# Scan outputs of two strips in one block, and the samples' memory values with exchanged operands

## The chip, the cores and the metric

The kernel runs on one core of a Trainium2 chip. The metric is the device time of one launch in microseconds (us), the median of several runs; smaller is better. A profile of one execution gives a trace of every engine: TensorE (PE, its weight loads PEld), VectorE (DVE), ScalarE (ACT), GpSimd (POOL) and the DMA queue of SyncE (SP).

## What is computed

One layer of a streaming encoder over 288 tokens (256 of a prompt, 32 of a sample), model width 2048: an RMS norm, one large projection, three branches (sparse attention, a Mamba-2 scan, cross-attention into 256 memory tokens), each gated and projected, their sum through an output matrix, a last norm. Two pieces matter here, cut from the reference:

```python
# the scan, chunks of up to 64 tokens, 32 heads of 64 in 4 groups, state 128
wgt = cb[..., None] * jnp.exp(seg) * dtc[:, :, None]
y_diag = jnp.einsum('bclsgr,bcsgrp->bclgrp', wgt, x)               # inside a chunk
y_off = jnp.einsum('bclgn,bcgrpn,bclgr->bclgrp', cc, h_in, jnp.exp(cum))   # from the state
y = y_diag + y_off
...
# memory attention
s = jnp.einsum('bthd,bmhd->bhtm', qh, mk) * (M_HEAD_DIM ** -0.5)
p = jax.nn.softmax(s, axis=-1)
o = jnp.einsum('bhtm,bmhd->bthd', p, mv)                           # the memory values
```

## The kernel before

**The stream.** Nearly all of the work is a stream of large products. A strip is 128 output channels; its weights come in halves of [128, 8, 128], loaded on SP's queue (line 183), split into a high part on ScalarE (line 186) and a low part on VectorE (line 187), and multiplied with the 288 tokens in 24 matmuls of 288 columns for a half (`strip`, `ps` tiles in PSUM). The order of the halves is a list, `jobs`, and `run` walks it: convert a later half, emit this half's matmuls, call `step`.

**Side work.** Everything else (attention, scan, scores) is written as generators. `step`, called after each half, advances the active ones to their next `yield`; at most `width` of them are active, others wait in `queue` in their order. So what a generator emits between two yields stands in each engine's queue between one half's matmuls and the next one's, as one block. Nothing reorders queues at run time but the waits. Side work uses PSUM tiles of the kind `sd` (five) and SBUF tiles of the kind `t2` (six).

**The scan** (`scan(g)`, one generator for each of four groups, one active at a time) holds the prompt's 256 tokens in two column blocks of 128 and the sample's 32 in a third (`COLS`). `Lt` has the masked decays, `xdt` the tokens' inputs, `hh` two states (for the prompt's second block, and for the sample), `C_` the output vectors. A group has four strips of 128 channels, two heads each. `out(j)` (lines 917 to 927) makes one strip's outputs in one PSUM tile: columns 0 to 288 from `xdt` and `Lt`, by block and head (64 output channels each, so half of the array's columns; for the third block only 32 of its rows), and columns 288 to 448 from `hh` and `C_`, with all 128 channels at once. `put(j)` (lines 929 to 934) reads them on VectorE and GpSimd. The calls: `out(0)`, `out(1)`, a yield, `put(0)`, `put(1)`, `out(2)`, `out(3)`, a yield, `put(2)`, `put(3)` and the states.

**The samples' memory attention** (`m_sample`, lines 456 to 481) has scores of four heads in four 32-row parts of one tile, a softmax, a transpose to `pt`, and then the values: for each head and each half of its 256 channels two accumulating matmuls with 128 channels of the cached values as weights and 32 columns of `pt` moving. Line 480 copies the result to `OTm`. It is one of the pieces that start behind the memory queries; the step sizes (`g_misc`), the index scores (`score`, two PSUM tiles for a pair of heads, read by line 590), `score_sample` and `select` follow in the queue, two active at a time.

An fp32 matmul of the program appears in the trace as two loads and two matmuls, one of fp32r (the stream) as one of each.

Of the kernel before, what the change touches and what calls it, by code (L numbers as in the profile page):

```python
# [9 lines left out]
AF = mybir.ActivationFunctionType  # L10
# [3 lines left out]
P = 128  # L14
# [9 lines left out]

# column blocks of the combined projection, in the order in which the kernel walks them
N_MQ, N_IQ, N_AK, N_AV, N_AQ, N_MZ, N_XBC, N_G = 8, 8, 2, 2, 8, 8, 24, 16
# [7 lines left out]
def step_kernel(ctx, tc, ins, outs):  # L34
# [17 lines left out]
    def sd():  # L52
        return psum.tile([P, 512], F32, tag="sd", bufs=5, name="sd")

    def t2(n=512):
        return tmp.tile([P, n], F32, tag="t2", name="t2")
# [10 lines left out]
    def mm(out, lhsT, rhs, start=True, stop=True):  # L67
        PE.matmul(out, lhsT, rhs, start=start, stop=stop)  # L68

    # ------------------------------------------------------------------ loads of the start  # L70
    N = Names()
# [27 lines left out]

    # ------------------------------------------------------------------ norms  # L100
    def rsqrt(v, p, n, size):
        """v = 1/sqrt(p / size + EPS), [128, n]; p in PSUM."""
        r, u = t2(n), t2(n)
        S.activation(r, p, AF.Ln, scale=1.0 / size, bias=eps)  # L104
        V.tensor_scalar(v, p, 1.0 / size, EPS, OP.mult, OP.add)
        S.activation(r, r, AF.Exp, scale=-0.5)
        V.scalar_tensor_tensor(u, r, -0.5, r, OP.mult, OP.mult)
        V.tensor_tensor(u, u, v, OP.mult)
        V.scalar_tensor_tensor(v, u, 1.5, r, OP.add, OP.mult)
# [14 lines left out]

    # ------------------------------------------------------------------ the streamed products
    jobs = []          # halves: (dram ap, shape, matmul emitter)
    conv = []          # converted halves that wait for their products
    state = {"c": 0}

    def strip(halves, mov, evac, n=T):  # L130
        """One block of 128 output channels; halves of its weights [128, 8, 128]."""
        box = {}
        for j, ap in enumerate(halves):
            def go(wh, wl, j=j):
                hi, lo = getattr(N, mov) if isinstance(mov, str) else mov
                if j == 0:
                    box["p"] = ps()
                p = box["p"][:, 0:n]
                k0 = 8 * j
                last = j == len(halves) - 1  # L140
                for i in range(8):
                    mm(p, wh[:, i], hi[:, k0 + i], j == 0 and i == 0, False)
                    mm(p, wh[:, i], lo[:, k0 + i], False, False)
                for i in range(8):
                    mm(p, wl[:, i], hi[:, k0 + i], False, last and i == 7)
                if last:
                    evac(p)
            jobs.append((ap, [P, 8, P], go))
# [20 lines left out]
    def hook(f):  # L169
        """f is called between the products before and after it."""  # L170
        jobs.append((None, None, f))
# [17 lines left out]

    # ------------------------------------------------------------------ side work  # L190
    queue, active = [], []
# [8 lines left out]
    def turn(key, gap):  # L200
        """Waits until gap halves have passed since the turn before this one."""
        while clock["t"] < clock.get(key, 0):
            yield
        clock[key] = clock["t"] + gap


    def later(*fs):
        """Each of fs one half further on than the one before it."""
        chains.append(list(fs))
# [44 lines left out]

    # ------------------------------------------------------------------ memory keys and values
    N.mkT = slot("E", [P, 8, 256])
# [109 lines left out]

    # ------------------------------------------------------------------ projections of the step
    wi = {"s": 0}
# [40 lines left out]

    # ---- memory attention  # L410

    def softmax(p, c, width_, scale):
        """Rows of p [128, c * width_]: c softmaxes; the maximum is subtracted."""
        m = st()
        V.tensor_reduce(m[:, 0:c], p.rearrange("p (i k) -> p i k", i=c), AX.X, OP.max, negate=True)
        V.tensor_scalar(m[:, 2:2 + c], m[:, 0:c], scale, None, OP.mult)
        e = t2()[:, 0:c * width_]
        for i in range(c):
            a = slice(i * width_, (i + 1) * width_)
            S.activation(e[:, a], p[:, a], AF.Exp, scale=scale, bias=m[:, 2 + i:3 + i],  # L420
                         accum_out=m[:, 4 + i:5 + i])
        V.reciprocal(m[:, 6:6 + c], m[:, 4:4 + c])
        for i in range(c):
            a = slice(i * width_, (i + 1) * width_)
            V.tensor_scalar(e[:, a], e[:, a], m[:, 6 + i:7 + i], None, OP.mult)
        return e
# [29 lines left out]
    def m_sample():  # L456
        p = sd()[:, 0:256]
        for h in range(4):
            for e in range(2):
                mm(p[32 * h:32 * h + 32], N.mqT[:, 2 * h + e, TP:T], N.cmk[:, 2 * h + e], e == 0, e == 1)  # L460
        yield
        e = softmax(p, 1, 256, 1.0 / 16)
        yield 2
        q = sd()[:, 0:256]
        for k in range(2):
            PE.transpose(q[:, k * P:k * P + P], e[:, k * P:k * P + P], ident)
        yield
        pt = t2()[:, 0:256]
        S.activation(pt, q, AF.Copy)
        yield  # L470
        o = sd()
        for h in range(4):
            for d in range(2):
                j = 2 * h + d
                for k in range(2):
                    c = h * 256 + d * P
                    mm(o[:, 32 * j:32 * j + 32], N.cmv[:, k, c:c + P], pt[:, k * P + 32 * h:k * P + 32 * h + 32],
                       k == 0, k == 1)
        yield
        S.activation(N.OTm[:, :, TP:T], o[:, 0:256].rearrange("p (j t) -> p j t", j=8), AF.Copy)  # L480
        mark("m")
# [7 lines left out]

    # ---- index keys, index weights, step sizes  # L490
    wt = const.tile([P, 3, 64], F32, name="wt")
# [13 lines left out]

    # columns of dts: step sizes, their products with -exp(a_log), running sums
    dt = const.tile([P, 96], F32, name="dt")
# [5 lines left out]
    def g_misc():  # L513
# [13 lines left out]
        mark("misc")  # L527
        # log(1 + exp(u)) = max(u, 0) + 2 atanh(e / (2 + e)), e = exp(-|u|)
        V.scalar_tensor_tensor(e, u, -1.0, u, OP.mult, OP.max)
# [40 lines left out]

    # ---- index scores
    def begin_a():
# [5 lines left out]
    def score(j):  # L578
        yield from need("misc")
        # a pair of heads, each in its own half of the rows of the array  # L580
        ps_ = [sd(), sd()]
# [104 lines left out]

    # ---- memory branch output
    def ev_mz(j, p):
# [12 lines left out]

    # ------------------------------------------------------------------ convolution, attention
    ASC = 128 ** -0.5
# [69 lines left out]
    cso = const.tile([P, 24, 6], F32, name="cso")  # L773
    # strips: the first group's channels, B, C, the other groups' channels
    order = list(range(4)) + list(range(16, 24)) + list(range(4, 16))
# [32 lines left out]

    # ------------------------------------------------------------------ memory gate; the scan
    def begin_scan():  # L810
# [14 lines left out]
    def scan(g):  # L825
# [28 lines left out]
        yield  # L854
        # x, token-major, times the step size
        px = []
# [16 lines left out]

        # decays from s to t
        def decay(*rs):
# [37 lines left out]
        yield 2  # L913
        # outputs
        po = []

        def out(j):
            p = sd()
            s = 4 * g + j
            po.append(p)  # L920
            for i, (c0, c1, n) in enumerate(COLS):
                for e in range(2):
                    r = 2 * j + e
                    mm(p[64 * e:64 * e + 64, c0:c1], xdt[0:n, i, 64 * r:64 * r + 64], Lt[0:n, r, c0:c1])
            cs = slice(P * s, P * s + P)
            mm(p[:, 288:416], hh[:, 0, cs], C_[:, 128:256])
            mm(p[:, 416:448], hh[:, 1, cs], C_[:, 256:288])

# [6 lines left out]

        out(0)
        out(1)
        yield
        put(0)
        put(1)  # L940
        ds = [ddx(1), ddx(2)]
        out(2)
        out(3)
        yield
# [24 lines left out]

    # ------------------------------------------------------------------ attention output  # L970
    def ev_az(j, p):
# [8 lines left out]

    # ------------------------------------------------------------------ scan output
    def begin_y():
# [76 lines left out]

    # ------------------------------------------------------------------ output product, last norm  # L1060
    POOLED = (2, 6, 9, 12, 14)
# [134 lines left out]
```

## Time and profile before

| | us |
|---|---|
| median of 3 runs | 1377.06 |
| lowest and highest run | 1375.69, 1378.71 |
| profiled execution: its span, first to last instruction | 1374.1 |

The profile gives no other time of that execution than its span. How to read it: an engine's busy time is the union of its instructions; matmuls are pipelined, so their durations overlap, and the distance between their starts is what one costs. A shape such as `128*64 128x128` is the used part of the array (rows times columns) and the moving data (partitions x columns). Times in a timeline are from the span's start; a row that merges several instructions carries the shape of the first. What stands in brackets is the idle time of the engine before, and what ended it.

### The profile page before, as it was taken

How to read it: one execution, taken by the hardware profiler on the slowest of the kernel's cores; microseconds unless marked ns; L12 is line 12 of the kernel's file. 1: busy time of each engine (PE TensorE's matmuls, PEld its weight loads, DVE VectorE, ACT ScalarE, POOL GpSimd, SP SyncE). 2: the span in 40 equal slices, each digit the busy share in tenths (PEclk: the TensorE clock that was granted, in tenths of full speed). 3: DMA queues.
4: the chain of work that ended last, by engine and by line, in shares of the span. 5: the costliest groups of instructions: out<-in, count | busy, mean ns of one | idle time of the engine just before them, and what ended most of it. 6: DMA issues, size and time to landing. Idle time of an engine off the chain costs nothing.

```text
span 1374.1 us, 24380 instructions
## 1 busy us (share of the span) xinstructions
PE 1347.9 (98%) x10032; PEld 1315.0 (96%) x10032; DVE 770.0 (56%) x1166; ACT 606.4 (44%) x858; POOL 237.5 (17%) x319
## 2 busy tenths in 40 slices
PE   6999999999999999999999999999999999999995
PEld 6989999899999999999999999999999999999995
DVE  7674344594567766646556556663344334555444
ACT  5654343444555543725425336663333433334331
POOL 5501000000000001122231233410044000000433
PEclk9999999999999999999999999999999999999998
DMA  8667434344444445654545445445456555455552
GB/s 288 212 217 255 143 130 132 118 162 158 165 139 151 151 156 164 224 181 146 179 136 186 165 156 167 159 164 172 166 170 218 173 169 166 157 169 169 170 169 84
DMA packets 63006, 232.03 MB, mean 169 GB/s; under 512 B 7264, under 2 KB 7808, under 8 KB 61744
## 3 DMA queue, kind: packets, MB, share of 16 engines
q1 hardware_dynamic: 57888, 209.72, 46.2%
q0 software_dynamic: 4144, 19.30, 4.3%
q8 instruction: 78, 1.28, 0.4%
q10 hardware_dynamic: 864, 1.47, 0.3%
q14 instruction: 32, 0.26, 0.1%
HBM read 223.06 MB, written 7.33 MB: 168 GB/s over the span
## 4 chain that ended last, share of the span: by engine, by line
PE 98%; DVE 1%; DMA 1%; ACT 0%; issue 0%; DVEq 0%; SPq 0%; ACTq 0%
PE ps L68 91%; PE sd L68 6%; DMA A<-in_memT 1%; DVE A L1089 0%; PE sd L861 0%; DVE C L268 0%; PE sd L727 0%; PE sd L845 0%; PE sd L440 0%; DVEq L1174 0%; ACT B L267 0%; ACT F L314 0%; PE sd L671 0%; ACT t L104 0%; ACT t L590 0%
## 5 line engine op out<-in xcount | busy, mean ns | idle before, releaser
L187 DVE TENSOR_TENSOR wl<-wr,wh 128x1024 fp32r<-128x1024 f32 x394 | 493.4, 1257 | 392.0 <-ACT wh L186 391.2
L68 PE MATMUL ps<-xh,wh 128*128 128x288 f32 x2128 | 582.2, 299 | 0.0
L68 PE MATMUL ps<-xl,wh 128*128 128x288 f32 x2128 | 574.5, 296 | 0.0
L186 ACT ACTIVATE wh<-wr 128x1024 fp32r<-128x1024 f32 x394 | 411.9, 1054 | 239.4 <-PE ps L68 194.8
L68 PEld LDWEIGHTS ps<-xh,wh 128*128 128x128 f32 x2128 | 400.3, 188 | 7.1 <-issue 3.4
L68 PEld LDWEIGHTS ps<-xl,wh 128*128 128x128 f32 x2128 | 400.6, 188 | 1.3 <-issue 0.7
L68 PE MATMUL ps<-xh,wl 128*128 128x288 f32 x2128 | 324.5, 294 | 0.0
L68 PEld LDWEIGHTS ps<-xh,wl 128*128 128x128 f32 x2128 | 296.6, 188 | 0.0
L68 PE MATMUL ps<-B,wh 128*128 128x288 f32 (+1 forms) x384 | 102.9, 296 | 9.3 <-ACT wh L186 9.3
L68 PEld LDWEIGHTS ps<-B,wh 128*128 128x128 f32 x384 | 74.2, 193 | 9.3 <-ACT wh L186 9.3
L68 PE MATMUL ps<-E,wh 128*128 128x288 f32 x256 | 70.2, 302 | 0.0
L68 PE MATMUL ps<-F,wh 128*128 128x288 f32 x256 | 69.5, 296 | 0.0
L68 PE MATMUL ps<-A,wh 128*128 128x288 f32 x256 | 69.2, 299 | 0.0
L68 PE MATMUL ps<-mgl,wh 128*128 128x288 f32 x256 | 69.1, 296 | 0.0
L68 PE MATMUL ps<-mgh,wh 128*128 128x288 f32 x256 | 69.0, 295 | 0.0
L790 POOL COPY cso<-t 128x3 f32<-128x3 f32 x24 | 5.0, 210 | 256.9 <-ACT t L788 256.9
L68 PEld LDWEIGHTS ps<-E,wh 128*128 128x128 f32 x256 | 48.3, 189 | 1.0 <-issue 0.8
L68 PEld LDWEIGHTS ps<-F,wh 128*128 128x128 f32 x256 | 48.1, 188 | 0.2 <-issue 0.2
L68 PEld LDWEIGHTS ps<-A,wh 128*128 128x128 f32 x256 | 48.3, 189 | 0.0
L68 PEld LDWEIGHTS ps<-mgl,wh 128*128 128x128 f32 x256 | 48.2, 188 | 0.0
L68 PEld LDWEIGHTS ps<-mgh,wh 128*128 128x128 f32 x256 | 48.1, 188 | 0.0
L68 PE MATMUL ps<-A,wl 128*128 128x288 f32 x256 | 39.3, 296 | 0.0
(290 smaller groups left out, 1348.5 us busy)
## 6 DMA issues: line engine op xcount, KB each, us to landing
wr<-in_w_in SPq DMA_DIRECT2D x266, 512.0 KB, 3.4
wr<-in_w_pb SPq DMA_DIRECT2D x32, 512.0 KB, 3.7
wr<-in_w_o SPq DMA_DIRECT2D x32, 512.0 KB, 3.3
wr<-in_w_mk SPq DMA_DIRECT2D x16, 512.0 KB, 3.8
wr<-in_w_mv SPq DMA_DIRECT2D x16, 512.0 KB, 4.3
wr<-in_w_pm SPq DMA_DIRECT2D x16, 512.0 KB, 3.3
wr<-in_w_pa SPq DMA_DIRECT2D x16, 512.0 KB, 3.3
B<-scr POOLq DMA_DIRECT2D x4, 1152.0 KB, 9.4
```

What stands on the lines that cost most here:

```text
L68: PE.matmul(out, lhsT, rhs, start=start, stop=stop)
L186: S.activation(wh, raw, AF.Copy)
L187: V.tensor_tensor(wl, raw, wh.bitcast(F32), OP.subtract)
L790: G.tensor_copy(cso[:, c, 0:3], u[:, 256:259])
```

## The change

In `scan`, `out` takes two strips: it first takes both PSUM tiles, then for each strip the first two blocks of `Lt` and, by heads, the state's outputs, with 64 weight columns instead of 128, and then for both strips the third block. In `m_sample` the weights of the value matmuls are now 32 columns of `pt` and the moving data 256 channels of the cached values, each head in its own 32 rows of the result; a copy to SBUF, a yield, two transposes, a yield and a rearranging copy bring it to the old form. Other lines of the diff only take comments away.

```diff
@@ m_sample
-        o = sd()
-        for h in range(4):
-            for d in range(2):
-                j = 2 * h + d
-                for k in range(2):
-                    c = h * 256 + d * P
-                    mm(o[:, 32 * j:32 * j + 32], N.cmv[:, k, c:c + P], pt[:, k * P + 32 * h:k * P + 32 * h + 32],
-                       k == 0, k == 1)
-        yield
-        S.activation(N.OTm[:, :, TP:T], o[:, 0:256].rearrange("p (j t) -> p j t", j=8), AF.Copy)
+        o = sd()[:, 0:256]
+        for k in range(2):
+            for h in range(4):
+                a = k * P + 32 * h
+                mm(o[32 * h:32 * h + 32], pt[:, a:a + 32], N.cmv[:, k, 256 * h:256 * h + 256], k == 0, k == 1)
+        yield
+        u = t2()[:, 0:256]
+        S.activation(u, o, AF.Copy)
+        yield
+        q = sd()[:, 0:256]
+        for d in range(2):
+            PE.transpose(q[:, d * P:d * P + P], u[:, d * P:d * P + P], ident)
+        yield
+        S.activation(N.OTm[:, :, TP:T].rearrange("p (h d) t -> p d h t", d=2),
+                     q.rearrange("p (d h t) -> p d h t", d=2, h=4), AF.Copy)
...
@@ scan
-        def out(j):
-            p = sd()
-            s = 4 * g + j
-            po.append(p)
-            for i, (c0, c1, n) in enumerate(COLS):
+        def out(*js):
+
+            for j in js:
+                po.append(sd())
+            for j in js:
+                for i, (c0, c1, n) in enumerate(COLS[0:2]):
+                    for e in range(2):
+                        r = 2 * j + e
+                        mm(po[j][64 * e:64 * e + 64, c0:c1], xdt[:, i, 64 * r:64 * r + 64], Lt[:, r, c0:c1])
+                for w, o, c0, c1 in ((0, 288, 128, 256), (1, 416, 256, 288)):
+                    for e in range(2):
+                        a = P * (4 * g + j) + 64 * e
+                        mm(po[j][64 * e:64 * e + 64, o:o + c1 - c0], hh[:, w, a:a + 64], C_[:, c0:c1])
+            for j in js:
                 for e in range(2):
                     r = 2 * j + e
-                    mm(p[64 * e:64 * e + 64, c0:c1], xdt[0:n, i, 64 * r:64 * r + 64], Lt[0:n, r, c0:c1])
-            cs = slice(P * s, P * s + P)
-            mm(p[:, 288:416], hh[:, 0, cs], C_[:, 128:256])
-            mm(p[:, 416:448], hh[:, 1, cs], C_[:, 256:288])
+                    mm(po[j][64 * e:64 * e + 64, 256:288], xdt[0:32, 2, 64 * r:64 * r + 64], Lt[0:32, r, 256:288])
...
-        out(0)
-        out(1)
+        out(0, 1)
         yield
         put(0)
         put(1)
         ds = [ddx(1), ddx(2)]
-        out(2)
-        out(3)
+        out(2, 3)
```

## Rows read from the trace of the kernel before

**Rows 1.** The page: busy time, share of the span and count of TensorE; the granted TensorE clock in 40 slices of the span, in tenths; and the shares of the engines in the chain of work that ended last.
```profile
PE 1347.9 (98%) x10032; PEld 1315.0 (96%) x10032; DVE 770.0 (56%) x1166; ACT 606.4 (44%) x858; POOL 237.5 (17%) x319
...
PEclk9999999999999999999999999999999999999998
...
PE 98%; DVE 1%; DMA 1%; ACT 0%; issue 0%; DVEq 0%; SPq 0%; ACTq 0%
```

**Rows 2.** The list of waits of TensorE over the whole span: what it waited for, us in total, times, longest.
```profile
PE ps L68 <- ACT wh L186: 9.3, 1, 9.3
...
PE sd L68 <- ACT t L590: 0.5, 1, 0.5
```

**Rows 3.** Busy time by engine in the stretch of the scan: from and to, length, then each engine's busy us and count, granted clock, DMA share, GB/s.
```profile
545.00:770.00 225.00, 225.00 (x1725) 211.11 (x1724) 130.94 (x247) 101.43 (x125) 57.20 (x66) 1.00 0.54 174
```

**Rows 4.** The timeline of TensorE and its weight loads through the first pair of strips, group 0, asked in short stretches so that runs come apart: start, us, what (the first row is the stream's last eight matmuls, the second the eighth of them); then two rows of VectorE from the same time.
```profile
586.12 1.22 PE L68 MATMUL ps<-xh,wl 128*128 128x288 f32 x8
587.05 0.29 PE L68 MATMUL ps<-xh,wl 128*128 128x288 f32 x1
587.27 0.33 PE L68 MATMUL sd<-B 128*64 128x128 f32 x2
587.43 0.39 PE L68 MATMUL sd<-B 128*64 128x128 f32 x4
587.65 0.46 PE L68 MATMUL sd<-B 128*64 128x128 f32 x4
587.86 0.30 PE L68 MATMUL sd<-B 32*64 32x32 f32 x4
587.93 0.23 PE L68 MATMUL sd<-B 32*64 32x32 f32 x2
588.09 0.38 PE L68 MATMUL sd<-G,A 128*128 128x128 f32 x1
588.30 0.42 PE L68 MATMUL sd<-G,A 128*128 128x128 f32 x3
588.41 0.31 PE L68 MATMUL sd<-G,A 128*128 128x32 f32 x2
588.45 0.28 PE L68 MATMUL sd<-G,A 128*128 128x32 f32 x1
588.65 0.33 PE L68 MATMUL sd<-B 128*64 128x128 f32 x2
...
590.15 0.29 PE L68 MATMUL ps<-xl,wh 128*128 128x288 f32 x1
...
587.27 0.14 PEld L68 LDWEIGHTS sd<-B 128*64 128x64 f32 x2 [0.16 <-issue]
587.32 0.25 PEld L68 LDWEIGHTS sd<-B 128*64 128x64 f32 x4
...
588.76 1.22 DVE L187 TENSOR_TENSOR wl<-wr,wh 128x1024 fp32r<-128x1024 f32 x1 [3.29 <-ACT wh L186]
589.90 0.51 DVE L931 SCALAR_TENSOR_TENSOR D<-D,cols,sd 128x288 f32<-128x288 f32 x1
```

**Rows 5.** The timeline of TensorE around the samples' memory values: the last stream matmul before, the values, the second stream matmul after.
```profile
232.00 0.29 PE L68 MATMUL ps<-xh,wl 128*128 128x288 f32 x1
232.13 3.65 PE L68 MATMUL sd<-t,A 128*128 128x32 f32 x32
...
235.84 0.29 PE L68 MATMUL ps<-xl,wh 128*128 128x288 f32 x1
```

**Rows 6.** The timeline of TensorE around the last pair of strips, group 3: the last stream matmul before it and the second after it.
```profile
760.49 0.29 PE L68 MATMUL ps<-xh,wl 128*128 128x288 f32 x1
...
763.60 0.29 PE L68 MATMUL ps<-xl,wh 128*128 128x288 f32 x1
```

**Rows 7.** The timeline of TensorE around the samples' memory scores, and around the two transposes of their softmax, with the stream matmuls before and after each.
```profile
214.09 0.29 PE L68 MATMUL ps<-xh,wl 128*128 128x288 f32 x1
214.32 1.09 PE L68 MATMUL sd<-A,G 128*32 128x256 f32 x16
215.34 0.40 PE L68 MATMUL ps<-xh,wh 128*128 128x288 f32 x1
215.58 0.29 PE L68 MATMUL ps<-xl,wh 128*128 128x288 f32 x1
...
225.40 0.30 PE L68 MATMUL ps<-xh,wl 128*128 128x288 f32 x1
225.53 0.38 PE L466 MATMUL sd<-ident,t 128*128 128x128 f32 x2
225.88 0.29 PE L68 MATMUL ps<-xl,wh 128*128 128x288 f32 x1
```

**Rows 8.** Single lines: the copy of line 469 (durations, first and last start); the last sum of the selection; the first attention head's scores; and two rows of the timeline of TensorE in the half of the last index score.
```profile
L469 ACT ACTIVATE t<-sd x1: 373/373/373, 227.3 to 227.3; 128x256 f32<-128x256 f32 x1
...
L646 DVE TENSOR_TENSOR C<-C x1: 726/726/726, 307.2 to 307.2; 128x544 f32<-128x544 f32 x1
...
357.10 0.82 PE L68 MATMUL sd<-C,B 128*128 128x128 f32 x4
...
263.62 0.49 PE L68 MATMUL sd<-C,B 64*128 64x128 f32 x2
264.57 0.92 PE L68 MATMUL sd<-C,B 64*128 64x128 f32 x6 [0.47 <-ACT t L590]
```

## The prediction

> **What bounds the kernel now.** I read the page's busy times first [rows 1]. TensorE's matmuls are busy 98% of the span, its granted clock is 9 tenths or more in every slice but the last, and the chain of work that ended last is TensorE's for 98%. Then the list of what TensorE waited for [rows 2]: its largest entry is 9.3 us, once, and that lies at the start. In the stretch of the scan it has no idle time at all [rows 3]. So a microsecond that TensorE loses or gains there moves the end by as much, and the other engines matter only where they would make it wait anew.
>
> A busy TensorE need not be a useful one, so the third view is the timeline around the changed steps, read by the starts of matmuls. The stream of 288-column products starts one every 0.133 us (eight from 586.12 to 587.05 [rows 4]). I price a block of side work as the time from the last stream matmul before it to the second one after it, less 0.27 us, which these two would be apart without it.
>
> **One pair of scan strips now.** From 587.05 to 590.15 us [rows 4] is 3.10, so the block costs 2.84 us. Its inside: two matmuls of the 128x64 shape start together every 0.11 us (587.43 to 587.65 is two steps; the first of a block holds 0.16), so both halves of the columns work at once. From the last of them to the first of 32x64 there are 0.20 us, from these to the first of 128x128 0.15. That first one holds 0.21 where later ones hold 0.11 (its load was not ahead), and from the last 32-column one to the next strip's 128x64 there are 0.20. The gaps stand only where the shape of the used part changes: at 232.00 to 232.13 the stream runs into side work of its own shape with no gap [rows 5]. A pair has six such changes. All eight pairs look alike: the last is 760.49 to 763.60, 3.11 [rows 6].
>
> **The pair after.** Per strip, four steps of two matmuls remain for the decayed part, and the state part, four full-width matmuls, becomes eight of half the width: two steps with 128 columns, two with 32. So a pair has 12 steps with 128 columns, 4 with 32, then 4 of 32x64, and three changes of shape. No row shows the 128x64 shape with 32 columns. Below it is bounded by the 0.03 between the 32-column starts at 588.41 and 588.45, above by the 0.11 of 128 columns. I take 0.06, because loads of 64 columns follow each other by 0.05 on each half (587.27 to 587.32) and a matmul can be no faster than its load. From the last stream matmul: 0.22 to the first start, 0.16 for the first step, 11 x 0.11 = 1.21, three 32-column steps 0.18, 0.15 into 32x64 (as after other 32-column matmuls; 0.20 at most), its steps 0.08 + 2 x 0.06, 0.16 to the first stream matmul, and 0.24 to the second (215.34 to 215.58, which follows a change too [rows 7]). That is 2.52, less 0.27: 2.25 us. Saved are 0.59 a pair, **4.7 us** for eight; with the bounds of the five 32-column steps and of the change, 2.3 to 5.9.
>
> Who could take this back? The first strip's outputs now come with the second's, at the end of the block and not in its middle. Their reader on VectorE (line 931) starts at 589.90, behind a weight conversion that began at 588.76 [rows 4]; by the sum the matmuls are over by about 589.5, so nobody waits for that. The masks that the outputs need are a whole half earlier, as now, and no other order of any queue changes here. Loads and conversions run ahead of the products through this stretch, so nothing else becomes late when TensorE needs 0.6 us less a pair.
>
> **The samples' memory values.** Now 32 matmuls with full-width weights and 32 moving columns, 0.11 us each: 232.00 to 235.84, cost 3.57 us [rows 5]. After: 16 matmuls with 32 weight columns in four parts of the array and 256 moving columns. The same function's scores have just this shape and count: 214.09 to 215.58, so 1.22 us. The way back is two transposes, like those at 225.53: 225.40 to 225.88, so 0.21 [rows 7]. Saved: 3.57 - 1.43 = **2.1 us**. The added read of the sums on ScalarE is another copy like line 469's, 0.37 us [rows 8], a half before the transposes need it; ScalarE stands behind no wait of TensorE there. Without that cover it would cost those 0.37.
>
> The generator gets two more yields, so all that queues behind it shifts. The eight index scores wait for its place among the two active pieces: they start two halves later and pack two to a half for one half longer, the later pieces one half later. The margin is large: selection's last sum ends at 307.9, and the first attention head that needs it starts at 357.10 [rows 8]. What can change is how often scores wait for PSUM tiles: at 263.62 one pair of scores began 0.95 us before its other six matmuls, which waited for the read of line 590. With two scores in that half this may come back larger, or disappear; between -0.9 and +0.9 us I take 0.
>
> **Sum.** 4.7 + 2.1 = 6.8 us of 1374.1, the profiled execution's span: 1367.3. The median of the runs stands 3.0 us above that span; nothing in the change touches what lies outside it, so 1377.06 - 6.8 = **1370.3 us**.
>
> **Rivals.**
> Slower: the half-width matmuls of the state part don't overlap, and each must wait for its own load. Its price is 0.21 a matmul, as for the first 128x128 one [rows 4]: per strip 8 x 0.21 = 1.7 instead of 0.34, in 16 strips 22 us, so 1370 + 22 = 1392. It undoes the whole saving from about 0.10 a matmul. For it speaks a change of stationary tensor within one shape, which no row here has. Against it: the loads at 587.32 start while the matmuls of 587.27, in the same 128 rows, still run, and two matmuls start together in each step.
> The Trainium skill says in "TensorE: Matmul & The Clock Gate", section "The mechanism" of Part 3, that a weight load overlaps a running matmul only when it is for another group of rows; by that rule the halves, which use all rows, would pay this price. The overlapping rows just named speak against the rule here, so it gets no more than a small chance.
>
> No gain in the scan: the 0.15 to 0.20 gaps follow the tensors (other weights, other tiles of PSUM) and not the shapes, so regrouping removes none. Then only the memory step gains: 1377.06 - 2.1 = 1375.0, no change that can be measured. Against it is the gapless entry at 232.13, where tile and weights change as well.
>
> Scores wait: the three halves with two scores each wait 0.95 us for PSUM as the one at 263.62 did, where now about half of that much is lost. That costs some 2 us: 1372. For it: the tiles of this kind are five, two scores take four. Against: the list of waits puts only 0.5 us on line 590 in all [rows 2].
>
> **Chances.** Forecast 0.80, scores wait 0.10, no gain in the scan 0.06, slower 0.04. The terms' own bounds give savings from 2.3 + 2.1 - 0.9 = 3.5 to 5.9 + 2.1 + 0.9 = 8.9, so 1368.2 to 1373.6. The ends together are unlikely, but the three runs of before already spread by 3 us: I take 1367.7 to 1373.4. It leaves out the two smallest rivals and little else. A difference of 0.2% (2.75 us) is about what a measurement can tell from none: faster 0.90, same 0.06, slower 0.04.
>
> **What would show it.** In the new profile each pair of strips should last about 2.5 us from the last stream matmul to the second after it, with two 128x64 starts every 0.11 through the state part, and just one 32x64 run. A step of 0.2 there shows the slower rival; a gap between runs of one shape the second. The memory values should be one run of 16 matmuls of 128x32, 1.2 us, and two transposes of 0.2 in a later half. New waits of TensorE for line 590 above 0.5 us would show the third. The prediction is wrong if TensorE gets idle time elsewhere that fills what it saves.

## The result and the profile after

The changed kernel takes **1368.57 us**, the median of four runs (1367.77 to 1369.36), beside 1376.58 for the kernel before (four runs, 1375.69 to 1378.71). The ratio is **0.994** (95% interval 0.9929 to 0.9952): 8.0 us less by the medians. The forecast was 1370.3 in a range of 1367.7 to 1373.4. In five later rounds (the experiment changed_again, below) it gave 0.9941 (0.9929 to 0.9954).

First the page and the list of waits of TensorE, as in [rows 1, 2]. The page's columns are busy time, share and count; the list's are what was waited for, us in total, times, longest.

```profile
PE 1341.2 (98%) x10082; PEld 1310.8 (96%) x10082; DVE 768.8 (56%) x1166; ACT 606.8 (44%) x859; POOL 238.3 (17%) x319
...
PEclk9999999999999999999999999999999999999998
```

```profile
PE ps L68 <- ACT wh L186: 8.5, 1, 8.5
...
PE sd L68 <- ACT t L595: 0.5, 1, 0.5
```

TensorE's busy time fell from 1347.9 to 1341.2 us though it has 50 more matmul passes: 64 more in the scan (the state part in halves), 14 fewer in the memory step. The span fell by 7.5, from 1374.1 to 1366.6. Behind the start no wait was added: the read of the index scores (line 595, formerly 590) still costs 0.5 us once.

The stretch of the scan as in [rows 3] (from and to, length, busy us and count of PE, PEld, DVE, ACT and POOL, granted clock, DMA share, GB/s):

```profile
545.00:770.00 225.00, 225.00 (x1827) 214.17 (x1826) 133.64 (x251) 103.42 (x127) 62.46 (x66) 1.00 0.53 177
```

It is as full as before, at the full clock (1.00 is the 2.4 GHz level). Busy time can't show the gain here; the starts of the matmuls can. The first pair of strips, with the same view and the same ends as in [rows 4], then one row of weight loads and two of VectorE (short stretches, so that runs come apart):

```profile
584.99 0.29 PE L68 MATMUL ps<-xh,wl 128*128 128x288 f32 x1
...
585.59 0.28 PE L68 MATMUL sd<-B 128*64 128x128 f32 x2
585.70 0.28 PE L68 MATMUL sd<-G,A 128*64 128x128 f32 x2
...
585.95 0.23 PE L68 MATMUL sd<-G,A 128*64 128x32 f32 x2
586.01 0.31 PE L68 MATMUL sd<-B 128*64 128x128 f32 x2
...
586.69 0.26 PE L68 MATMUL sd<-G,A 128*64 128x32 f32 x4
586.72 0.23 PE L68 MATMUL sd<-G,A 128*64 128x32 f32 x2
586.88 0.24 PE L68 MATMUL sd<-B 32*64 32x32 f32 x2
...
587.47 0.29 PE L68 MATMUL ps<-xl,wh 128*128 128x288 f32 x1
...
585.59 0.14 PEld L68 LDWEIGHTS sd<-G,A 128*64 128x64 f32 x2
...
586.71 1.23 DVE L187 TENSOR_TENSOR wl<-wr,wh 128x1024 fp32r<-128x1024 f32 x1 [3.29 <-ACT wh L186]
587.85 0.51 DVE L942 SCALAR_TENSOR_TENSOR D<-D,cols,sd 128x288 f32<-128x288 f32 x1
```

From 584.99 to 587.47 is 2.48 us, less 0.27: the block costs 2.21 where it cost 2.84. Two halves start together every 0.11. From the decayed part (out of B) to the state part (out of G, A) and back to the second strip there is no gap of the kind that stands between two shapes: weights, moving data and columns of PSUM change at 585.70 and 586.01, the used part of the array doesn't. One run of 32x64 is left, at the end. The conversion of the weights (line 187) ends at 587.94 by its own row, after the pair's last matmul, and the reader of the outputs (line 942) follows it: nobody waits for the first strip's outputs. There is one small price: the first step of the second strip holds 0.14 us where the others hold 0.11. All eight pairs cost 2.211 to 2.214 (taken with one more digit, where the two stream matmuls would be 0.266 apart).

The memory step, as in [rows 5, 7]: the values, the two transposes that turn them back, and the new copy on ScalarE.

```profile
232.15 0.29 PE L68 MATMUL ps<-xh,wl 128*128 128x288 f32 x1
232.37 1.07 PE L68 MATMUL sd<-A,t 128*32 128x256 f32 x16
...
233.62 0.29 PE L68 MATMUL ps<-xl,wh 128*128 128x288 f32 x1
...
241.25 0.30 PE L68 MATMUL ps<-xh,wl 128*128 128x288 f32 x1
241.38 0.38 PE L482 MATMUL sd<-ident,t 128*128 128x128 f32 x2
241.73 0.29 PE L68 MATMUL ps<-xl,wh 128*128 128x288 f32 x1
...
233.74 0.38 ACT L478 ACTIVATE t<-sd 128x256 f32<-128x256 f32 x1
```

The values cost 1.20 us (232.15 to 233.62, less 0.27) in place of 3.57, the transposes 0.22 (0.48 less 0.27, from starts with one more digit 0.219). The copy is over at 234.12 and the transposes start 7.26 us later.

**Where the time came from.** Eight pairs at 0.631 are 5.05 us, the memory step 3.570 - 1.198 - 0.219 = 2.15, together 7.2. TensorE's stretch, from the first matmul of the prompt's memory scores (160.44 us before, 160.59 after) to the last matmul of all, takes 1191.6 us instead of 1198.9: 7.3 less. The span's other 0.2 is what remains of two differences outside it. The stretch begins 0.15 us later, and behind its end there are 14.4 us instead of 14.8; both of these values come with either form of the kernel (scan_only has 14.4, pair_full_width 14.8). Of the further 0.5 between the span and the medians, 0.3 lies in the part of an execution's time that its span does not hold ("What stays open", below).

### The profile page after: what moved, and what is told of

Read it like the earlier page. It is cut to its first block, busy times and chain, and to the rows that moved or that the text cites. A ratio compares the mean times of both kernels' runs of the same rounds, so it can differ in the third digit from the quotient of the medians.

```text
span 1366.6 us, 24483 instructions
## 1 busy us (share of the span) xinstructions
PE 1341.2 (98%) x10082; PEld 1310.8 (96%) x10082; DVE 768.8 (56%) x1166; ACT 606.8 (44%) x859; POOL 238.3 (17%) x319
## 4 chain that ended last, share of the span: by engine, by line
PE 98%; DVE 1%; DMA 0%; ACT 0%; issue 0%; DVEq 0%; ACTq 0%
PE ps L68 91%; PE sd L68 5%; DVE C L268 0%; DVE A L1098 0%; PE sd L866 0%; DMA cols<-in_cols 0%; PE sd L732 0%; PE sd L850 0%; PE sd L440 0%; DVEq L1183 0%; ACT F L314 0%; PE sd L676 0%; ACT B L267 0%; ACT t L104 0%; ACT t L595 0%
## 5 line engine op out<-in xcount | busy, mean ns | idle before, releaser
(293 smaller groups left out, 1341.2 us busy)
```

## The experiments

Times here are of one run each unless rounds are named; the kernel before ran on the same chip. "Cost" of a block is always the time from the last stream matmul ahead of it to the second behind it, less 0.27 us (0.266 where a third digit is given). None of the kernels leaves out a part of the computation.

### Each part alone

**scan_only** has the new order of the scan's outputs and the old memory values; **mem_only** the reverse. The cut below is of scan_only against the changed kernel; mem_only is the kernel before with the new `m_sample`.

```diff
@@ m_sample
-        o = sd()[:, 0:256]
-        for k in range(2):
...
+        o = sd()
+        for h in range(4):
+            for d in range(2):
...
```

> The scan's part alone, memory values as before. Theory (each block of side work costs TensorE its own time and nothing gives it back): a pair of strips from the last stream matmul to the second one after it, less 0.27 us, 2.21 us as in the changed kernel, eight pairs 5.0 us less than before; the memory values still 3.57; the index scores start in the same halves as before, with TensorE waiting about 0.5 us once for line 590. Rival (the two parts share a gain, for example through the later scores): the pairs differ from 2.21, or the span differs from that of before by clearly more or less than 5 us.

> The memory values' part alone, scan outputs as before. Theory: one block of 16 matmuls for 1.2 us and one with two transposes for 0.22 in place of 3.57, so 2.1 us less; pairs of strips 2.84 as before; the blocks of the step sizes and index scores that shift behind it cost the same in sum within 0.3 us. Rival (scores wait): those blocks cost 1 to 2 us more, and the span gains less than 1 us.

scan_only took 1372.37 us beside 1375.98, mem_only 1373.0. The ends of the first pair of strips in mem_only, on TensorE's timeline:

```profile
584.61 0.29 PE L68 MATMUL ps<-xh,wl 128*128 128x288 f32 x1
...
587.72 0.29 PE L68 MATMUL ps<-xl,wh 128*128 128x288 f32 x1
```

The costs belong to the parts: a pair's ends are 3.11 us apart (cost 2.84) without the new order and 2.48 (2.21) in scan_only; the memory values cost 1.20 in mem_only and 3.57 in scan_only. In mem_only TensorE's stretch (from the prompt's memory scores to the last matmul) is 2.2 us shorter than before's, which is the memory step's 2.15; the blocks of step sizes and scores behind it last the same in sum, within 0.1 us. The rival by which the shifted scores wait falls.

scan_only missed its expected size: TensorE's stretch is 3.6 us shorter, not 5.05. The pairs gained what they should, so 1.5 us were lost elsewhere. They lie behind the memory values: from the first of these to the first matmul of the step sizes there are 8.28 us (232.30 to 240.58), and 6.76 in the kernel before (232.13 to 238.89). The granted clock shows how. Its windows around the old memory values (columns as above), then one of the kernel before behind the same values:

```profile
232.00:236.00 4.00, 4.00 (x37) 4.00 (x36) 3.68 (x9) 1.37 (x3) 0.00 (x0) 1.00 0.26 92
236.20:239.40 3.20, 3.20 (x15) 3.20 (x15) 0.00 (x0) 0.17 (x1) 0.00 (x0) 0.50 0.63 187
239.60:245.00 5.40, 5.40 (x45) 4.95 (x44) 1.22 (x1) 1.06 (x1) 0.00 (x0) 1.00 0.27 97
```

```profile
235.80:239.40 3.60, 3.60 (x30) 3.60 (x29) 0.25 (x1) 1.45 (x2) 0.00 (x0) 1.00 0.58 199
```

TensorE is never idle here, yet right behind the old values the clock stands at 0.50 (the 1.2 GHz level) for 3.4 us: 15 matmuls in 3.20 us where before's profiled execution has 30 in 3.60. This code is the same in both kernels. Whether the old values bring it about is the question of old_values_twice, below.

### What in the pair gains

**halves_one_strip** keeps the halves and gives up putting two strips together.

```diff
-        out(0, 1)
+        out(0)
+        out(1)
...
-        out(2, 3)
+        out(2)
+        out(3)
```

> The changed kernel, but one strip at a time: the state part by halves of the columns, the third block of each strip right behind it. Five changes of shape a pair instead of three (six before). Theory (a change of shape costs what the gaps of before show, the halves' loads are hidden): 2.43 us a pair, so the halves alone give 0.41 of the 0.63 us that a pair gains, taking two strips together 0.22. Rival A (all of the gain is from taking two strips together): 2.8. Rival B (all of it is from the halves): 2.2.

```profile
586.08 0.29 PE L68 MATMUL ps<-xh,wl 128*128 128x288 f32 x1
...
588.79 0.29 PE L68 MATMUL ps<-xl,wh 128*128 128x288 f32 x1
```

1371.26 us, and a pair costs 2.71 - 0.27 = 2.44 (2.446 to 2.454 over the eight). So the halves by themselves save 0.39 a pair, and one run of 32x64 in place of two a further 0.24. Neither of the rivals' values (2.8: only the grouping counts; 2.2: only the halves) came.

**pair_full_width** keeps two strips together and, at the end, the state part in full width, so that there are as few changes of shape as in the changed kernel.

```diff
...
+            for j in js:
+                cs = slice(P * (4 * g + j), P * (4 * g + j) + P)
+                mm(po[j][:, 288:416], hh[:, 0, cs], C_[:, 128:256])
+                mm(po[j][:, 416:448], hh[:, 1, cs], C_[:, 256:288])
```

> The changed kernel with two strips together, but the state part in full width, behind the third blocks: 128x64 for both strips, then 32x64, then 128x128. Three changes of shape, as in the changed kernel, and none into the stream. Theory (changes of shape and loads that are not hidden both count): the first load of 128x128 is exposed once (0.21) and eight full-width loads follow at 0.11 each, 2.45 us a pair. Rival (only the number of changes counts): 2.2 or less, since the change into the stream is gone too.

```profile
586.77 0.29 PE L68 MATMUL ps<-xh,wl 128*128 128x288 f32 x1
...
588.37 1.08 PE L68 MATMUL sd<-G,A 128*128 128x128 f32 x8
...
589.50 0.30 PE L68 MATMUL ps<-xl,wh 128*128 128x288 f32 x1
```

1372.42 us; the pair costs 2.73 - 0.27 = 2.46. The number of shape changes alone does not set the price: eight full-width loads, of which the first is not ahead, cost 0.25 more than the same work in halves, where the 32-column steps come at 0.03 and 0.06.

### The memory step's own questions

**memory_head_outer** puts a head's two steps next to each other, so that four neighbours in the queue no longer lie in four parts of the array.

```diff
-        for k in range(2):
-            for h in range(4):
+        for h in range(4):
+            for k in range(2):
```

> The changed kernel with the loops over heads and halves of the memory exchanged in the memory values: the two accumulating matmuls of a head follow each other, as in the same function's scores. Theory (each of the four column parts takes its own next matmul, whatever stands between in the queue): one block of 1.20 us as in the changed kernel. Rival (matmuls run in the queue's order, so neighbours must lie in different parts to overlap): up to 16 x 0.216 = 3.5 us.

```profile
232.21 0.29 PE L68 MATMUL ps<-xh,wl 128*128 128x288 f32 x1
...
233.70 0.29 PE L68 MATMUL ps<-xl,wh 128*128 128x288 f32 x1
```

1368.37 us; 1.49 - 0.27 = 1.22 us, from starts with one more digit 1.218 beside 1.198. The order costs 0.02 us. The rival of 3.5 (neighbours must lie in different parts) falls.

**no_yield_before_turn** takes away the yield between the copy of the values and their transposes.

```diff
         S.activation(u, o, AF.Copy)
-        yield
         q = sd()[:, 0:256]
```

> The changed kernel without the yield between the copy of the memory values and the two transposes, so that both lie in one half. Theory (the yield hides more than the copy): TensorE waits there for what ScalarE has queued ahead, a weight conversion of 1.05 us, and for the copy of 0.37 us, so the transposes' block costs 0.22 plus 0.4 to 1.8 us; the pieces behind shift by one half less. Rival (only the copy counts, or ScalarE is free): 0.22 to 0.6 us in all.

```profile
233.64 0.38 ACT L478 ACTIVATE t<-sd 128x256 f32<-128x256 f32 x1
...
236.57 0.38 PE L481 MATMUL sd<-ident,t 128*128 128x128 f32 x2
```

1368.18 us, and no wait: the copy is over at 234.02, and the transposes start at 236.57. The half of the stream between the values and the next side work is cover enough. The transposes joined the block of step sizes (1.739 us with them, 1.519 alone) and TensorE's stretch is 1191.55 beside 1191.57. My theory of a new wait of 0.4 to 1.8 us falls, and with it the prediction's remark that the copy would cost its 0.37 without the added half: the added yield hides nothing that was not hidden.

**old_values_twice** is scan_only with the old values computed two times into the same place, to see whether it is these matmuls that let the clock fall.

```diff
+        for again in range(2):
             for h in range(4):
                 for d in range(2):
```

> The kernel with the scan's part alone and the memory values of before, whose 32 matmuls are computed twice, the second time over the first. Theory (the old form, 32 moving columns for every load of 128, uses the array so little that TensorE's granted clock can fall to its lower level behind it, as in the profile of the kernel with the scan's part alone, where 3.4 us at half the clock stand behind the block and cost 1.5 us): with 7.1 us of such matmuls on end the clock falls in or behind the block, and the stream's matmuls there start every 0.24 us or so in place of 0.133. Rival (the fall of the clock in that one profile had nothing to do with the block): the clock stays at 1.00 through and behind it, and only 3.55 us are added.

Its values and the first stream matmuls behind them, then its windows:

```profile
231.92 9.70 PE L68 MATMUL sd<-t,A 128*128 128x32 f32 x64
241.82 0.44 PE L68 MATMUL ps<-xl,wh 128*128 128x288 f32 x1
242.06 0.44 PE L68 MATMUL ps<-xh,wh 128*128 128x288 f32 x1
```

```profile
231.90:236.20 4.30, 4.30 (x42) 4.30 (x40) 3.42 (x8) 1.36 (x2) 0.00 (x0) 1.00 0.37 122
236.40:241.40 5.00, 5.00 (x25) 5.00 (x25) 0.00 (x0) 0.00 (x0) 0.00 (x0) 0.50 0.31 105
...
246.60:250.00 3.40, 3.40 (x29) 2.94 (x29) 1.23 (x1) 0.12 (x1) 0.00 (x0) 1.00 0.14 35
```

1378.81 us beside 1375.62. After some 4.4 us of these matmuls the clock falls to 0.50, in the midst of them, and stays there until 246.5, 10.2 us in all; the stream's matmuls start every 0.24 instead of 0.133. This is what the theory asked for, and the rival falls; that little use of the array is the reason, as the theory has it, is not shown by it. What TensorE did before the fall: full-width weights with 32 moving columns each, one every 0.11, no idle time. That the old form can cost more than its own 3.57 us is shown by these two kernels; none of the eleven profiles of kernels with the new memory values has a fall there. That it sometimes happens in the kernel before itself is not shown. Of its 35 executions that are on record with their spans, the four longest (1375.2 and 1375.3 us; the middle one has 1374.2) have a mean granted clock of 0.994 or 0.995, most of the others 0.996: that would fit such a fall, but no trace of them is kept.

### Going further in the same direction

**third_block_padded** computes the last 32 tokens' step with all 128 rows, the missing ones zero, so that a pair has no change of shape inside.

```diff
+        G.memset(N.xdt[:, 2], 0.0)          # begin_scan
-                for i, (c0, c1, n) in enumerate(COLS[0:2]):
+                for i, (c0, c1, n) in enumerate(COLS):
...
-                    mm(po[j][64 * e:64 * e + 64, 256:288], xdt[0:32, 2, 64 * r:64 * r + 64], Lt[0:32, r, 256:288])
```

> The changed kernel with the third block in the same shape as the rest: its 32 rows are padded to 128, the unused rows of the samples' inputs set to zero once at the scan's start, so the 128x64 shape holds for the whole pair. Theory (a change of shape costs, rows of the array do not): two changes of shape fewer take 0.36 us of 32x64 work away and put 0.23 us of the same steps in, 2.09 us a pair in place of 2.21, 1.0 us less in all, 1367.6 against 1368.6. Rival (a matmul over 32 rows is cheaper than over 128): 2.2 us or more a pair, no gain.

```profile
585.00 0.29 PE L68 MATMUL ps<-xh,wl 128*128 128x288 f32 x1
...
587.37 0.29 PE L68 MATMUL ps<-xl,wh 128*128 128x288 f32 x1
```

1367.64 us (five rounds, 1367.13 to 1368.33), ratio 0.9937 (0.9924 to 0.9949). A pair costs 2.10, a further 0.11 less, and TensorE's stretch is 0.9 us shorter than in the changed kernel (the intervals of the two ratios overlap): multiplying by zeros in the shape that is already set is cheaper here than a smaller shape.

**four_strips_padded** adds to this all four strips of a group in one block.

```diff
-        out(0, 1)
+        out(0, 1, 2, 3)
...
-        out(2, 3)
```

> The padded version with all four strips of a group in one block; the reads of the third and fourth strip stay a half later. Theory: per group one entry and one exit of the shape fewer, 3.86 us in one block instead of 2 x 2.09, so 1.3 us less over four groups, 2.3 us less than the changed kernel, about 1366.3. Rival (four tiles of five held for two halves make TensorE wait for PSUM): new idle time of TensorE before the states' matmuls, and no gain over the padded version.

```profile
704.34 2.18 PE L68 MATMUL sd<-t,t 128*128 128x512 f32 x4 [1.18 <-DVE ev L941]
```

1367.46 us (five rounds, 1367.23 to 1368.48), ratio 0.9938 (0.9925 to 0.9952). A block of four costs 3.87, so four of them gain 1.3 us over eight padded pairs, but in the third group the matmuls that follow wait 1.18 us for VectorE's reads of the outputs (line 941), which now come in one heap, and the states' block costs 3.56 us instead of 2.11. TensorE's stretch is 0.15 us longer than with padded pairs: the gain turned into a new wait, as the rival had it.

**four_strips_read_at_once** reads all four outputs in one half, to have the tiles free sooner (the cut is against four_strips_padded).

```diff
         yield
-        put(0)
-        put(1)
+        for j in range(4):
+            put(j)
         ds = [ddx(1), ddx(2)]
         yield
-        put(2)
-        put(3)
```

> The padded version with all four strips in one block, and all four reads in the half right behind it. Theory (the one new wait of 1.2 us that four strips in a block brought, for line 941 in the third group, came from the late reads of the third and fourth strip): that wait is gone, four blocks of 3.87 us stay, side work of TensorE 1.3 us less than in the padded version with pairs and 2.2 us less than in the changed kernel; about 1366.4 where the changed kernel has 1368.6. Rival (VectorE, with four reads and a conversion in one half, becomes late): TensorE waits for line 187 or 941 in that half and the gain goes.

It took 1373.31 us (five rounds, eleven runs, 1371.31 to 1375.13), ratio 0.998 (0.9971 to 0.9989). The third group's states, the four additions and the scaling on GpSimd ahead of them and the conversion beside, on the timeline; then windows:

```profile
706.90 3.08 PE L68 MATMUL sd<-t,t 128*128 128x512 f32 x4 [3.51 <-POOL t L877]
...
701.49 3.34 POOL L942 TENSOR_TENSOR D<-D,ev 128x160 f32<-128x160 f32 x4 [16.11 <-DVE ev L941]
704.79 2.05 POOL L877 TENSOR_TENSOR t<-B,dde 128x512 f32<-128x512 f32 x1
704.73 1.22 DVE L187 TENSOR_TENSOR wl<-wr,wh 128x1024 fp32r<-128x1024 f32 x1
```

```profile
706.00:707.00 1.00, 0.10 (x1) 0.10 (x1) 0.00 (x0) 0.00 (x0) 1.00 (x2) 1.00 0.89 352
...
708.90:711.00 2.10, 2.10 (x6) 1.09 (x5) 0.00 (x0) 0.00 (x0) 0.94 (x1) 0.50 0.16 64
```

The theory fell. The two scalings of line 877, which the states need, are queued on GpSimd behind four additions instead of two; TensorE waits 3.51 us, and after that the clock is granted at 0.50. The states' block costs 6.96 us instead of 2.11.

**four_strips_scaled_first** issues the scalings ahead of the yield, before anything that waits for outputs (the cut is against four_strips_read_at_once).

```diff
         out(0, 1, 2, 3)
+        ds = [ddx(1), ddx(2)]
         yield
         for j in range(4):
             put(j)
-        ds = [ddx(1), ddx(2)]
```

> The version with four strips in a block and all reads behind it, with the two scalings of the inputs on GpSimd (ddx) issued a half earlier, behind the outputs' matmuls and ahead of the four additions. Theory (the 3.5 us that TensorE waited in the third group came from these scalings standing behind the four additions in GpSimd's queue, and the slower matmuls behind that wait from its clock): that wait is gone in all groups, the states' block costs 2.1 us in the third group too, and the side work is 2.2 us less than in the changed kernel, some 1366.2 where that has 1368.4. Rival (VectorE's four reads and its conversions in one half of the third group are late themselves): TensorE waits for line 187, 941 or GpSimd by a microsecond or more in that group.

```profile
703.73 2.07 PE L68 MATMUL sd<-t,t 128*128 128x512 f32 x4
```

**1366.48 us** (five rounds, 1365.8 to 1366.57), ratio **0.9927** (0.9913 to 0.994): the fastest of all. The states at 703.73 wait for nothing, a block of four costs 3.87, and TensorE's stretch is 1189.4 us, 2.2 less than in the changed kernel. The intervals of this ratio and of the changed kernel's still overlap; the order of the two rests on the traces and on the runs' ranges.

**changed_again** is the changed kernel once more, in five rounds.

> The changed kernel itself, timed beside the version with four strips in a block on one chip: 6.8 us of side work less than before, so about 0.5% faster, and some 2 us slower than the version with four strips. The reason to run it is that times of single runs differ by more than these 2 us.

1368.23 us (1367.95 to 1369.03) beside 1376.27 for the kernel before, ratio 0.9941 (0.9929 to 0.9954), span 1366.5.

## Why the prediction was right, step by step

**The bound.** TensorE without idle time sets the end: the two blocks' 7.2 us are nearly all of the 7.3 of its stretch and of the span's 7.5. Shown by each part alone too, but for scan_only, where the granted clock took 1.5 us of 5.05.

**The pair of strips.** The mechanism was right in both its parts (halves 0.39, grouping 0.24, together 0.63). The term was a little small: 4.7 predicted, 5.05 measured. The mis-sized step is that of the 32-column matmuls. I took 0.06 for each of three; they came at 0.03, 0.06 and 0.03 (586.69 to 586.72 is one such interval). The reason given, that a matmul can be no faster than its load, does not hold for a single step: these steps' loads are 0.06 apart. That makes 0.06 less a pair; 0.03 of it goes back in the first step of the second strip (0.14 instead of 0.11) and 0.01 in the change into 32x64 (0.16 instead of 0.15). So a pair ends 0.04 earlier, 0.3 us for eight.

**The slower rival** falls. The loads of the state part start at 585.59, while the decayed part's matmuls of 585.59 run, and the first matmuls on them start 0.11 later. The rule of the Trainium skill that the prediction set against the trace ("TensorE: Matmul & The Clock Gate", section "The mechanism" of Part 3: a load overlaps a running matmul only when it is for other rows) is not what these rows show for the 128x64 shape. In pair_full_width, where the weights are of full width and the shape changes, the first load is not ahead: the first matmul holds 0.21 there (588.37 to 588.58).

**No gain in the scan** falls: the gaps go with the shape, not with the tensors (585.70 has new weights and new moving data, 586.01 a new tile of PSUM as well, and neither has such a gap). third_block_padded confirms it by taking out the last inner change.

**The memory values.** 1.43 predicted, 1.42 measured; the row of the scores was the right price. The copy on ScalarE cost nothing, as said. Wrong was the price named for the cover's loss: without the added half it still cost nothing, as the half of the stream that follows the values hides it.

**Scores wait** falls. The later place of the scores gave neither the 2 us nor a gain: the list of waits has the same 0.5 us. In the half with two scores and a wait, the row is this, and the block's price in sum with its neighbours is before's:

```profile
259.73 0.49 PE L68 MATMUL sd<-C,B 64*128 64x128 f32 x2
260.69 1.69 PE L68 MATMUL sd<-C,B 64*128 64x128 f32 x14 [0.47 <-ACT t L595]
```

The 0.96 us between the two starts are those of [rows 8], once, in a half of two scores instead of one.

**What stays open.** The medians moved by 8.0, the span by 7.5. Of the difference, 0.3 goes with the memory step: in all 40 executions on record of kernels with the new one the time stands 1.65 to 1.81 us above the span, in all 37 with the old one 1.97 or more (2.03 in the middle). Why is not shown. The prediction took 3.0 us for this distance, the median of three runs less the one span that it had, and held that the change leaves it alone; neither came true. The median came out 1.7 us below the forecast: 0.7 is the span (1366.6, not 1367.3), 1.3 this distance (1.7, not 3.0), less 0.3, as the profiled execution (1368.28) lies under its median. So the mechanism was right and the span nearly so, but it is the width of the range that took in the error of this term. And how often the kernel before itself pays for a fallen clock was not settled: its own trace has 1.00 there, scan_only's has 0.50.

## What to carry to other kernels

On a TensorE that is always busy, price side work by the starts of its matmuls from one stream matmul to another: in these kernels gaps of 0.15 to 0.2 us stand where the used part of the array changes, so order the work by that part, split wide matmuls or pad small ones to stay in it, and exchange operands so that few weight columns meet many moving ones. When such a gain enlarges a block, look at the queue of the engine that reads or feeds it next: four strips at once gained nothing until the scalings that TensorE needs were issued ahead of the additions that only wait for it. Test each part alone and look at the granted clock before adding up the parts' gains.

## What the runs showed of the hardware that was not expected

**A busy TensorE can lose its clock.** With full-width weights and 32 moving columns, one matmul every 0.11 us and no idle time, the granted clock fell from 1.00 to 0.50 behind 3.5 us of them in scan_only (for 3.4 us), and after some 4.4 us of them in old_values_twice (for 10.2 us); the kernel before, with the same matmuls, kept 1.00 in its profiled execution.

**GpSimd's scaling takes twice as long where a conversion on VectorE has started before it.** Line 877 in four_strips_read_at_once, by durations (lowest, median, highest, in ns):

```profile
L877 POOL TENSOR_TENSOR t<-B,dde x12: 1032/1038/2054, 560.5 to 763.6; 128x512 f32<-128x512 f32 x8, 32x512 f32<-32x512 f32 x4
```

The longest, 2.05 us, is the one at 704.79 in the timeline above, which starts behind the conversion of 704.73 (two inputs in SBUF); the median is 1.04. Where the scaling starts first, it keeps its time and the conversion takes longer, 1.93 us instead of 1.22. From the same run's timeline:

```profile
592.12 1.03 POOL L877 TENSOR_TENSOR t<-B,dde 32x512 f32<-32x512 f32 x1
592.37 1.93 DVE L187 TENSOR_TENSOR wl<-wr,wh 128x1024 fp32r<-128x1024 f32 x1 [1.88 <-ACT wh L186]
```

The kernel before has a slow case too: 2.02 us at 761.10, behind a conversion of 760.90. The Trainium skill says in "SBUF — State Buffer", section "Who interferes with whom", that a VectorE instruction with two inputs in SBUF contends with GpSimd's reads; these rows agree.

**The order of four column parts hardly matters.** Sixteen matmuls of 128x32 take 1.20 us when neighbours in the queue lie in four parts and 1.22 when they lie in the same one.
